# PEER decoding with the sixteen choices innermost, index rows spread by ScalarE, in the slot of spent scores

## The chip, the cores and the metric

The kernel runs on one core of one Trainium2 chip. The metric is the device time of one execution in microseconds (us); the kernel before takes 2549.07 us, the median of 3 runs (2547.81 to 2551.14). Engines: PE is TensorE (matmuls; PEld its weight loads), DVE is VectorE, ACT is ScalarE, POOL is GpSimd, SP is SyncE, which here only issues DMAs.

## The reference

One layer of a hybrid block for 1024 tokens of width 1024. First two mixers (an RG-LRU and an S5 scan) and an output product are added to the residual. Then comes PEER, a product-key lookup of experts, 128 per token (8 heads by 16) out of 16384:

```python
q = (xb @ wq).reshape(TOK_BLOCK, PEER_HEADS, PEER_QDIM)
s1 = einsum('thd,kd->thk', q[..., :PEER_HALF], k1)
s2 = einsum('thd,kd->thk', q[..., PEER_HALF:], k2)
v1, i1 = lax.top_k(s1, 16)
v2, i2 = lax.top_k(s2, 16)
cand = v1[..., :, None] + v2[..., None, :]          # 16 x 16 per head
sc, cidx = lax.top_k(cand.reshape(..., 256), 16)
e = take_along_axis(i1, cidx // 16) * 128 + take_along_axis(i2, cidx % 16)
g = softmax(sc)
act = gelu(einsum('thkd,td->thk', u_tab[e], xb))
out = einsum('thk,thkd->td', g * act, v_tab[e])
```

The change is in the line `e = ...`: of each head, sixteen chosen positions cidx are turned into indices by looking each one up in a list of sixteen (i1 and i2). This is called the decode below.

## The kernel before, in words

The mixers take the first 440 us of the profiled execution. The rest is `peer`. The 1024 tokens are 8 blocks of 128 (a token to a partition), worked in two ways:

- Blocks 5 to 7 are *gathered*. For each of a token's 128 experts POOL's indirect DMA (`ask`, L1380) fetches a row of u, and later of v, for all 128 tokens of the block at once; DVE multiplies and adds (tiles `row`, `act`, `hb`). These are 768 units of one DVE product each, and eight row buffers.
- Blocks 0 to 4 (640 tokens) are *dense*: PE computes all experts. The first product `ap` needs the split weights `uh` (ACT) and `ul` (DVE) of the loaded `ur` (L1461); its gelu goes to the tile `aa` (ACT) and, for 97 of 128 expert tiles, is stored ahead to DRAM (`A_d`, L1559). A half of such a tile is a *step* of 24 matmuls. The weights of the chosen experts are made for every four tokens (a *group*, in `build`) from one-hots `ohA` (DVE) and `ohB` (DVE and ACT) by matmuls `gp`; eight groups fill a tile `gs`, which four DMAs store to `G_d` (L1325). The one-hots of a block need the tile `kt`, the block's transposed indices and weights. After all groups the dense loop runs, which reads `A_d` and `G_d` back.

Which experts a token gets is found as follows. `query` multiplies the tokens by the query weights (loaded as `wqr`, split into `wqh` by ACT and `wql` by DVE; the matmuls `qp`), part 0 for the gathered blocks, part 1 for the dense ones, and makes scores `sp`, 256 per head. Block 0's scores are copied by ACT into the tile `s` (tag "s" of pool `pk`, one buffer, 8 KB a partition), a head at a time; those of blocks 1 to 4 go to DRAM (`S_d`) and are loaded back into the same tile `s` later, 1 MB each (L1205). The largest sixteen of each half are searched by DVE (`top16`: MAX8, FIND_INDEX8 and MATCH_REPLACE8, five operations for one row of 128): `found_g` for the gathered blocks, `search0` for block 0, and the loop in `topk` for blocks 1 to 4. `topk(b)` goes on with 80 candidate sums (`cd`), their top sixteen, a softmax (`ex`), and the chosen positions in the two lists (`pa_`, `pb_`). Then for each of the two halves comes the decode: an `is_equal` of each position with 0 to 15 (`i16`), a multiplication by the sixteen indices `ib`, and four adds that sum over the sixteen (8, 4, 2 and 1 wide), the last into the f32 tile `if`. The tile `oh` of 128 choices by 16 has a slot of its own (4 KB).

The order of the instructions is set by `Merge`, which interleaves generators by modelled costs while the kernel is built: a generator yields, with a condition where it must wait (`search0` waits for a head's scores), and the one whose modelled time is lowest goes on. The framework's scheduler then orders each engine by priority and readiness, also ahead of the chip. On the chip each engine runs its fixed row of instructions in order. `choose` runs `topk` for the dense blocks: block 0's by count of steps, block n's so that its k-th part comes at group 32(n-1)+k. `topks` runs it for the gathered blocks. `build` lets group g go once 23+g steps are done. All engine operations are recorded under L146, a helper's line, so tiles are the names to go by.

Of the kernel before, what the change touches and what calls it, by code (L numbers as in the profile page):

```python
# [9 lines left out]
BF = mybir.dt.bfloat16  # L10
I32 = mybir.dt.int32
U32 = mybir.dt.uint32
AF = mybir.ActivationFunctionType
ALU = mybir.AluOpType
# [4 lines left out]
P = 128  # L19
# [9 lines left out]
def bc(ap, pos, n):  # L29
    shape = list(ap.shape)  # L30
    v = ap.unsqueeze(pos)
    shape.insert(pos, n)
    return v.to_broadcast(shape)
# [1008 lines left out]
def peer(tc, a, cst, pools, h, nx, mg):  # L1042
# [3 lines left out]
    V, S, G, PE = mg.V, mg.S, mg.G, mg.PE  # L1046
    ident, iota = cst["ident"], cst["iota"]
# [103 lines left out]
    def top16(x, vals, at, pin=False):  # L1151
        for r in range(2):
            vs = vals[:, 8 * r:8 * r + 8]
            ins = V.max(vs, x)
            if pin and r == 0:
                tc.keep_in_program_order(ins)
            V.max_index(at[:, 8 * r:8 * r + 8], vs, x)
            if r == 0:
                V.match_replace(x, vs, x, -3.0e38)
# [18 lines left out]
    gp = pools.open("gp", "right", bufs=2)  # L1178
    pu = pools.open("pu", "right", bufs=2)
    pk = pools.open("pk", "right", bufs=1)  # L1180
    i16 = pk.tile([P, 16], BF, name="i16")
    V.tensor_copy(i16, iota[:, 0:16])


    def search0():
# [11 lines left out]
    def topk(b):  # L1197
        if b >= ND:
            yield "found"
            v, ix = found[b - ND]  # L1200
        elif b == dblocks[0]:
            v, ix = s0.pop()
        else:
            s = pk.tile([P, 8, 2, P], F32, name="s", tag="s", bufs=1)
            nc.sync.dma_start(s, S_d[b].rearrange("p h (f k) -> p h f k", f=2))  # L1205
            mg.at(mg.dma(1024))
            yield
            v = pk.tile([P, 2, 8, 16], F32, name="v", tag="v")
            ix = pk.tile([P, 2, 8, 16], U32, name="ix", tag="ix")
            for h in range(8):  # L1210
                for f in range(2):
                    top16(s[:, h, f], v[:, f, h], ix[:, f, h])
                yield

        cd = pk.tile([P, 8, 80], F32, name="cd", tag="cd")
        v1, v2 = v[:, 0], v[:, 1]
        V.tensor_tensor(cd[:, :, 0:16], v2, v1[:, :, 0:1].to_broadcast([P, 8, 16]), ALU.add)
        V.tensor_tensor(cd[:, :, 16:72].rearrange("p h (a b) -> p h a b", b=8), bc(v1[:, :, 1:8], 3, 8),
                        bc(v2[:, :, 0:8], 2, 7), ALU.add)
        V.tensor_tensor(cd[:, :, 72:80], v1[:, :, 8:16], v2[:, :, 0:1].to_broadcast([P, 8, 8]), ALU.add)  # L1220
        sc = pk.tile([P, 8, 16], F32, name="scv", tag="scv")
        ci = pk.tile([P, 8, 16], U32, name="ci", tag="ci")
        for h in range(8):
            top16(cd[:, h], sc[:, h], ci[:, h])
            yield

        ex = pk.tile([P, 8, 16], F32, name="ex", tag="ex")
        V.tensor_tensor(ex, sc, sc[:, :, 0:1].to_broadcast([P, 8, 16]), ALU.subtract)
        yield
        S.activation(ex, ex, AF.Exp)  # L1230
        yield
        sm = pk.tile([P, 8], F32, name="sm", tag="sm")
        V.tensor_reduce(sm, ex, AX.X, ALU.add)
        V.reciprocal(sm, sm)
        g = gw[b - ND].rearrange("p (h k) -> p h k", k=16) if b >= ND else \
            pk.tile([P, 8, 16], F32, name="gd", tag="gd")
        V.tensor_tensor(g, ex, bc(sm, 2, 16), ALU.mult)

        ri = pk.tile([P, P], I32, name="ri", tag="ri")
        cif = ci.rearrange("p h k -> p (h k)").bitcast(I32)  # L1240
        V.tensor_scalar(ri, cif, 3, None, ALU.arith_shift_right)
        V.tensor_scalar(cif, cif, 7, None, ALU.bitwise_and)
        rf = pk.tile([P, P], F32, name="rf", tag="rf")
        cf = pk.tile([P, P], F32, name="cf", tag="cf")
        t9 = pk.tile([P, P], F32, name="t9", tag="t9")
        V.tensor_copy(rf, ri)
        V.tensor_copy(cf, cif)
        V.scalar_tensor_tensor(t9, rf, 9.0, cf, ALU.is_equal, ALU.mult)
        V.tensor_tensor(cf, cf, t9, ALU.subtract)
        pa_ = pk.tile([P, P], BF, name="pa_", tag="pa")  # L1250
        pb_ = pk.tile([P, P], BF, name="pb_", tag="pb")
        t1 = ri.bitcast(F32)
        V.tensor_scalar(t1, rf, 1.0, 8.0, ALU.is_equal, ALU.mult)
        V.tensor_tensor(pb_, cf, t1, ALU.add)
        V.tensor_scalar(rf, rf, -1.0, 0.0, ALU.add, ALU.max)
        V.tensor_tensor(pa_, rf, t9, ALU.add)
        yield
        ib = pk.tile([P, 2, 8, 16], BF, name="ib", tag="ib")
        V.tensor_copy(ib, ix)
        res = []  # L1260
        for f, pos in ((0, pa_), (1, pb_)):
            oh = pk.tile([P, P, 16], BF, name="oh", tag="oh")
            V.tensor_tensor(oh, bc(pos, 2, 16), bc(i16, 1, P), ALU.is_equal)
            oh4 = oh.rearrange("p (h k) a -> p h k a", k=16)
            yield
            V.tensor_tensor(oh4, oh4, bc(ib[:, f], 2, 16), ALU.mult)
            yield
            for m in (8, 4, 2):
                V.tensor_tensor(oh[:, :, 0:m], oh[:, :, 0:m], oh[:, :, m:2 * m], ALU.add)
            o = pk.tile([P, P], F32, name=f"if{f}", tag=f"if{f}")  # L1270
            V.tensor_tensor(o, oh[:, :, 0], oh[:, :, 1], ALU.add)
            res.append(o)
            yield
        return res[0], res[1], g

    def topk_gather(b):
        i1, i2, g = yield from topk(b)
        n = b - ND
        V.scalar_tensor_tensor(i1, i1, 128.0, i2, ALU.mult, ALU.add)
        V.tensor_copy(idx[n], i1)  # L1280
        mg.flag(f"g{n}")
        yield
# [4 lines left out]
    kts, groups, steps = {}, [0], [0]  # L1287

    def choose():
        for n, b in enumerate(dblocks):  # L1290
            found_ = topk(b)
            k = 0
            while True:
                try:
                    next(found_)
                except StopIteration as e:
                    i1, i2, g = e.value
                    break
                k += 1
                at = P // 4 * (n - 1) + k if n else BEGIN + RATE * k  # L1300
                yield lambda: (groups if n else steps)[0] >= at
            p_ = pt("gt")
            for m, x in enumerate((i1, i2, g.rearrange("p h k -> p (h k)"))):
                PE.transpose(p_[:, m * P:(m + 1) * P], x, ident)
            yield
            kt = pk2.tile([P, 5, P], F32, name="kt", tag="kt", bufs=KT)
            V.tensor_copy(kt[:, 0:3], p_[:, :3 * P].rearrange("p (a b) -> p a b", b=P))
            V.tensor_scalar(kt[:, 3:5], kt[:, 1:3], -1.0, None, ALU.mult)
            kts[b] = kt
            mg.flag(f"k{b}")  # L1310
            yield
        mg.flag("k")
# [273 lines left out]

    pace[0] = PACE
    mg.add([(0.0, build()), (0.0, choose()), (1.0, ahead())])
    mg.run([], until="k")
    pools.close("pk")  # L1590
# [283 lines left out]
def body(tc, a):  # L1874
    nc = tc.nc
    pools = Pools(tc)
    pcst = pools.open("cst")
    ident = pcst.tile([P, P], F32, name="ident")
    make_identity(nc, ident)
    iota = pcst.tile([P, P], F32, name="iota")  # L1880
    nc.gpsimd.iota(iota, pattern=[[1, P]], base=0, channel_multiplier=0, allow_small_or_imprecise_dtypes=True)
    mg = Merge(nc)
    cst = dict(ident=ident, iota=iota)
    fpools, h, nx = front(tc, a, cst, ND, mg)
    peer(tc, a, cst, fpools, h, nx, mg)
    pools.close("cst")
# [65 lines left out]
```

## Time and profile before

| | us |
|---|---|
| median of 3 runs | 2549.07 |
| the profiled execution | 2566.11 |
| its span | 2564.3 |
| PE busy | 2490.0 |
| DVE busy | 2361.0 |
| ACT busy | 1336.8 |
| POOL busy | 1193.1 |

The profiled execution is 0.7% longer than the median of the timed ones. In the profile each instruction is named by its engine, its operation and the tiles it writes and reads (`oh<-oh,ib`), with partitions by elements and the element type; a group of equal ones by count, busy us and mean ns of one. A wait `A <- B` is idle time of an engine ahead of instructions that write A, ended by B.

### The profile page before, as it was taken

The page shows a single profiled execution, that of the slowest core. Times are in us where ns is not written, and L with a number is a line of the kernel's source. Part 1 is how long each engine was busy: PE and PEld are TensorE (multiplying, and loading weights), DVE is VectorE, ACT ScalarE, POOL GpSimd, SP SyncE. Part 2 cuts the span into 40 slices and gives each one's busy share as a digit, 9 for nine tenths or more (in the row PEclk, how much of TensorE's full clock was granted, in tenths as well). Part 3 has the DMA queues.
Part 4 walks back from the last instruction along what each step waited for, and adds up shares of the span by engine and source line. Part 5 has one row for each costly group of instructions (what it writes and reads, how often), then busy time and mean ns, then how long its engine had stood idle before and what let it go on. Part 6 is the DMA issues. An engine that isn't in the chain of part 4 may idle for free.

```text
span 2564.3 us, 40749 instructions
## 1 busy us (share of the span) xinstructions
PE 2490.0 (97%) x14639; PEld 2258.2 (88%) x14639; DVE 2361.0 (92%) x4496; ACT 1336.8 (52%) x2388; POOL 1193.1 (47%) x853
## 2 busy tenths in 40 slices
PE   9999999999999999999999999999999999999997
PEld 8777889999989989999999888888888888888886
DVE  8899569999999999999977699999999999999998
ACT  6667334333577777777877344343344344333442
POOL 4000000364467575566555465555556556555551
PEclk9899999999999999999999999999999999999999
DMA  5113124677899989999999999999999999999994
GB/s 191 30 41 130 58 93 157 205 261 271 285 384 328 361 301 324 349 349 310 386 350 351 355 375 356 348 353 356 357 351 367 357 356 351 349 360 355 348 354 150
DMA packets 300906, 750.68 MB, mean 293 GB/s; under 512 B 29600, under 2 KB 127072, under 8 KB 296096
## 3 DMA queue, kind: packets, MB, share of 16 engines
q0 software_dynamic: 112896, 411.09, 43.8%
q1 hardware_dynamic: 185280, 334.19, 36.9%
q10 hardware_dynamic: 2528, 2.80, 0.3%
q8 instruction: 115, 1.88, 0.3%
q14 instruction: 87, 0.71, 0.1%
HBM read 661.87 MB, written 84.93 MB: 291 GB/s over the span
## 4 chain that ended last, share of the span: by engine, by line
PE 61%; DVE 28%; DMA 5%; issue 4%; ACT 2%; POOL 0%; SPq 0%; DVEq 0%; ACTq 0%; POOLq 0%
PE vp L146 26%; PE ap L146 18%; PE total L146 7%; DVE hb L146 5%; PE wop L146 3%; DVE row L146 3%; DVE ul L146 2%; PE gp L146 2%; PE qp L146 2%; DVE ohA L146 2%; DVE oh L146 1%; DMA ur<-in_uT_dram 1%; DVE ix L146 1%; DVE v L146 1%; DVE ci L146 1%
## 5 line engine op out<-in xcount | busy, mean ns | idle before, releaser
L1380 POOL DMA_INDIRECT row<-in_peer_u_dram,idx x384 | 589.1, 1534 | 665.1 <-DVE scv L146 243.8
L1380 POOL DMA_INDIRECT row<-in_peer_v_dram,idx x384 | 567.6, 1478 | 450.7 <-DVE hb L146 264.6
L146 PE MATMUL ap<-xDl,uh 128*128 128x320 f32 x2048 | 649.4, 317 | 7.4 <-ACT aa L146 7.3
L146 PE MATMUL ap<-xDh,ul 128*128 128x320 f32 x2048 | 635.7, 310 | 4.4 <-DVE ul L146 4.4
L146 PE MATMUL ap<-xDh,uh 128*128 128x320 f32 x2048 | 635.1, 310 | 0.0
L146 DVE SCALAR_TENSOR_TENSOR hb<-row,act,hb 128x1024 f32<-128x1024 f32 x384 | 492.5, 1283 | 10.7 <-DMA row<-in_peer_v_dram,idx 5.8
L146 DVE CUSTOM_DVE_ANT_0 row<-row,xg 128x1024 f32<-128x1024 f32 x384 | 458.5, 1217 | 5.1 <-DMA row<-in_peer_u_dram,idx 4.8
L146 PE MATMUL vp<-vl,hh 128*128 128x512 f32 x1024 | 398.8, 389 | 0.0
L146 PE MATMUL vp<-vh,hl 128*128 128x512 f32 x1024 | 398.7, 389 | 0.0
L146 PE MATMUL vp<-vh,hh 128*128 128x512 f32 x1024 | 398.6, 389 | 0.0
L146 PEld LDWEIGHTS ap<-xDl,uh 128*128 128x128 f32 x2048 | 387.9, 189 | 10.2 <-ACT aa L146 9.1
L146 PEld LDWEIGHTS ap<-xDh,ul 128*128 128x128 f32 x2048 | 387.5, 189 | 6.7 <-DVE ul L146 5.4
L146 PEld LDWEIGHTS ap<-xDh,uh 128*128 128x128 f32 x2048 | 386.9, 189 | 0.0
L146 ACT ACTIVATE gq<-gt 128x640 f32<-128x640 f32 x128 | 174.7, 1365 | 318.3 <-DVE hr L146 302.5
L146 PEld LDWEIGHTS vp<-vh,hh 128*128 128x128 f32 x1024 | 192.2, 188 | 40.2
L146 PEld LDWEIGHTS vp<-vl,hh 128*128 128x128 f32 x1024 | 192.2, 188 | 39.3 <-issue 0.4
L146 PEld LDWEIGHTS vp<-vh,hl 128*128 128x128 f32 x1024 | 192.2, 188 | 38.8
L146 ACT ACTIVATE ohB<-ohB,kt 128x128 f32<-128x128 f32 x480 | 201.6, 486 | 0.0
L146 PE MATMUL gp<-ohB,ohA 128*128 128x128 f32 x1280 | 172.7, 278 | 20.6 <-DVE ohB L146 14.0
L146 PEld LDWEIGHTS gp<-ohB,ohA 128*128 128x128 f32 x1280 | 160.8, 192 | 28.4 <-issue 10.4
L146 DVE TENSOR_TENSOR ul<-ur,uh 128x1024 fp32r<-128x1024 f32 x128 | 155.8, 1218 | 22.7 <-ACT uh L146 22.7
L146 ACT ACTIVATE aa<-ap 128x320 f32<-128x320 f32 x194 | 84.4, 436 | 175.3 <-PE ap L146 170.0
(451 smaller groups left out, 4466.5 us busy)
## 6 DMA issues: line engine op xcount, KB each, us to landing
ur<-in_uT_dram SPq DMA_DIRECT2D x128, 512.0 KB, 6.5
vr<-in_peer_v_dram SPq DMA_DIRECT2D x128, 512.0 KB, 7.0
gt<-G_d SPq DMA_DIRECT2D x32, 1280.0 KB, 10.1
G_d<-gs SPq DMA_DIRECT2D x79, 512.0 KB, 10.6
A_d<-aa SPq DMA_DIRECT2D x96, 320.0 KB, 7.4
hr<-A_d SPq DMA_DIRECT2D x96, 320.0 KB, 6.0
wqr<-in_wq_dram SPq DMA_DIRECT2D x31, 512.0 KB, 3.7
row<-in_peer_u_dram,idx POOLq DMA_INDIRECT x384, 7.6
```

What stands on the lines that cost most here:

```text
L146: return fn(*args, **kw)
L1380: G.indirect_dma_start(out=r, out_offset=None, in_=a["peer_v" if at >= P else "peer_u"], in_offset=bass.IndirectOffsetOnAxis(ap=idx[n][:, ...
```

## The change

The decode's tile is turned round, and moved:

- The tile of a half is now [8 heads, 16 slots, 16 choices]: the sixteen choices of a head lie innermost, and the sixteen list positions (slots) outside them. `ia` holds each number 0 to 15 sixteen times over; the compare takes the positions `pos` as they lie, repeated over the slots.
- ACT spreads the sixteen indices of each head over the choices (`ibx`, 128x2048, bf16), once for each half: the first time ahead of `cd`, the second between the first half's multiplication and its adds. The cast to `ib` comes earlier. The multiplication is of two whole tiles.
- The four adds sum over the slots, in runs of sixteen choices.
- `oh` and `ibx` together take 8 KB under the tag "s": the one buffer that holds the scores of block 0 and then those of blocks 1 to 4. The 4 KB of the old tile `oh` are gone.
- In `choose`, block n from 1 on begins its `topk`, whose first instruction is the load of its scores, only at group 32(n-1)-2.

```diff
-    i16 = pk.tile([P, 16], BF, name="i16")
-    V.tensor_copy(i16, iota[:, 0:16])
+    ia = pk.tile([P, 16, 16], BF, name="ia")
+    V.tensor_copy(ia, bc(iota[:, 0:16], 2, 16))
...
+        ib = pk.tile([P, 2, 8, 16], BF, name="ib", tag="ib")
+        V.tensor_copy(ib, ix)
+        both = pk.tile([P, 2, 8, 16, 16], BF, name="oh", tag="s", bufs=1)
+        oh, ibx = both[:, 0], both[:, 1]
+        S.activation(ibx, bc(ib[:, 0], 3, 16), AF.Copy)
         cd = pk.tile([P, 8, 80], F32, name="cd", tag="cd")
...
-        ib = pk.tile([P, 2, 8, 16], BF, name="ib", tag="ib")
-        V.tensor_copy(ib, ix)
         res = []
         for f, pos in ((0, pa_), (1, pb_)):
-            oh = pk.tile([P, P, 16], BF, name="oh", tag="oh")
-            V.tensor_tensor(oh, bc(pos, 2, 16), bc(i16, 1, P), ALU.is_equal)
-            oh4 = oh.rearrange("p (h k) a -> p h k a", k=16)
-            yield
-            V.tensor_tensor(oh4, oh4, bc(ib[:, f], 2, 16), ALU.mult)
-            yield
+            V.tensor_tensor(oh, bc(pos.rearrange("p (h k) -> p h k", k=16), 2, 16), bc(ia, 1, 8), ALU.is_equal)
+            yield
+            V.tensor_tensor(oh, oh, ibx, ALU.mult)
+            yield
+            if f == 0:
+                S.activation(ibx, bc(ib[:, 1], 3, 16), AF.Copy)
             for m in (8, 4, 2):
                 V.tensor_tensor(oh[:, :, 0:m], oh[:, :, 0:m], oh[:, :, m:2 * m], ALU.add)
             o = pk.tile([P, P], F32, name=f"if{f}", tag=f"if{f}")
-            V.tensor_tensor(o, oh[:, :, 0], oh[:, :, 1], ALU.add)
+            V.tensor_tensor(o.rearrange("p (h k) -> p h k", k=16), oh[:, :, 0], oh[:, :, 1], ALU.add)
...
         for n, b in enumerate(dblocks):
             found_ = topk(b)
             k = 0
+            if n:
+                yield lambda: groups[0] >= P // 4 * (n - 1) - 2
             while True:
```

(`bc(x, pos, n)` repeats x over a new axis of length n at place pos.) The whole order of the instructions shifts with this: since `oh` is now a tile of the tag "s", the copy of block 0's first scores stands behind the last add of block 5's decode; the decode of blocks 6 and 7, which lay among the queries' products, stands behind the last search of block 0's scores; block 1's load of scores stands behind the last add of block 0's decode; and the loads of blocks 2 to 4 stand behind a set of four stores to `G_d` rather than ahead of it. Blocks 5 and 0 keep their places to within a few instructions, and the dense loop's order is the same.

## Prediction

> **What bounds the kernel now.** First the page's head and its busy times, then the engines' busy times by stage, because this kernel has stages with different limits.
>
> ```profile
> span 2564.3 us, 40749 instructions
> PE 2490.0 (97%) x14639; PEld 2258.2 (88%) x14639; DVE 2361.0 (92%) x4496; ACT 1336.8 (52%) x2388; POOL 1193.1 (47%) x853
> core 0: us, PE busy (x) PEld busy (x) DVE busy (x) ACT busy (x) POOL busy (x), PEclk, DMA share, GB/s
> 440.00:592.00 152.00, 146.48 (x1006) 143.27 (x1006) 148.01 (x558) 47.79 (x99) 66.40 (x41) 0.99 0.64 217
> 592.00:659.00 67.00, 62.64 (x422) 61.57 (x422) 67.00 (x237) 17.97 (x28) 27.61 (x21) 1.00 0.84 291
> 659.00:760.00 101.00, 94.07 (x642) 91.84 (x641) 95.58 (x254) 66.83 (x160) 67.06 (x45) 0.97 0.96 350
> 760.00:1245.00 485.00, 469.01 (x3344) 462.81 (x3343) 478.93 (x1159) 377.37 (x908) 297.93 (x166) 1.00 0.96 335
> 1245.00:1450.00 205.00, 201.94 (x1448) 201.10 (x1447) 149.96 (x252) 143.75 (x337) 102.73 (x71) 1.00 1.00 355
> 1450.00:2564.00 1114.00, 1098.88 (x5378) 947.65 (x5377) 1058.45 (x1206) 447.23 (x500) 594.97 (x426) 0.99 0.93 345
> ```
>
> The stages are the rest of the queries (440 to 592 us), block 0's choice (to 659), block 0's routing groups (to 760), the choices of blocks 1 to 4 (to 1245), groups alone (to 1450), and the dense loop. From 1245 on PE is busy for 201.94 of 205 us and 1098.88 of 1114, so nothing that VectorE saves there can shorten the run. In the four stages ahead, where all the decoding lies, both engines are nearly full: VectorE is idle for 152 + 67 + 101 + 485 less 148.01, 67.00, 95.58 and 478.93, which is 15.5 us, and PE for 5.5 + 4.4 + 6.9 + 16.0 = 32.8 us. PE's 32.8 us are the most that a lighter VectorE can give back. Whether it does depends on the waits, of which PE's largest in the groups' stages (690 to 1260 us) are these, with total, count and mean or longest in us:
>
> ```profile
> PE gp L146 <- DVE ohB L146: 14.0, 20, 2.5
> PE gp L146 <- ACT ohB L146: 5.2, 3, 3.3
> ```
>
> PE does wait for VectorE, by 14 us at the one-hots ohB, and ACT's own ohB holds it up for 5.2 us more.
>
> **The change part by part.** *1, the decode on VectorE.* A half decode is a compare, a multiplication and four adds. The groups by shape (busy us, mean ns), and the first and last of the sixteen compares (minimum, median and maximum ns):
>
> ```profile
> L146 DVE TENSOR_TENSOR oh<-oh,ib 128x2048 bf16<-128x2048 bf16 x16 | 19.7, 1233 | 0.0
> L146 DVE TENSOR_TENSOR oh<-oh 128x1024 bf16<-128x1024 bf16 x16 | 11.1, 694 | 0.0
> L146 DVE TENSOR_TENSOR oh<-oh 128x256 bf16<-128x256 bf16 x16 | 7.7, 480 | 0.0
> L146 DVE TENSOR_TENSOR oh<-oh 128x512 bf16<-128x512 bf16 x16 | 7.6, 472 | 0.0
> L146 DVE TENSOR_TENSOR if<-oh 128x128 f32<-128x128 bf16 x16 | 7.0, 435 | 0.0
> L146 DVE TENSOR_TENSOR oh<-pa__4501,i x1: 2282/2282/2282, 465.3 to 465.3; 128x2048 bf16<-128x2048 bf16 x1
> L146 DVE TENSOR_TENSOR oh<-pb__13460,i x1: 2290/2290/2290, 1229.7 to 1229.7; 128x2048 bf16<-128x2048 bf16 x1
> ```
>
> The compare takes 2.28 us and the multiplication of the same 2048 bf16 elements 1.23. The compare's first operand repeats one position over its innermost run; after the change every operand of both steps over neighbouring bf16 elements, so I give the compare the multiplication's row: 1.05 us less. The adds of 1024 and 512 differ by 222 ns for 512 elements, 0.43 ns each; carried on from 472 ns this gives 0.36 us for 256, where the row shows 0.48 (runs of two): 0.12 less. The last add reads single elements two apart and takes 0.435; by the same step neighbours would take some 0.31: 0.13 less. The add of 512 I leave, but for 0.02. So 1.05 + 0.02 + 0.12 + 0.13 = 1.32 us a half, and for 8 blocks by 2 halves 21 us. Bounds: nothing at all if the comparison doesn't speed up and short runs don't matter, and 24 us if all adds gain. I take 21, since the multiplication's row is the same size and type.
>
> The Trainium skill, "VectorE: DVE Perf Modes", What auto-detection actually checks, says that two elements a cycle need every tensor to be 16-bit with step one, and names no length of the run. By it the 256 add was fast already and the last add, which writes f32, never is, so 16 times 1.05 = 16.8 us would go and the sum below be 4 us higher. The 480 ns beside 472 for twice the elements speaks against it for short runs.
>
> *2, ACT's sixteen spreads of 128x2048.* No row shows one. The nearest on both sides:
>
> ```profile
> L146 ACT ACTIVATE wqh<-wqr 128x1024 fp32r<-128x1024 f32 x31 | 32.6, 1052 | 1.5 <-DMA wqr<-in_wq_dram 1.5
> L146 ACT ACTIVATE gq<-gt 128x640 f32<-128x640 f32 x128 | 174.7, 1365 | 318.3 <-DVE hr L146 302.5
> ```
>
> Doubling the first less one fixed part gives 1.9 to 2.1 us; at the second's 2.13 ns an element it would be 4.4 us. I take 2, for the elements read lie side by side in bf16: 32 us in all, half of them (four blocks) between 760 and 1245 where ACT is busy for 377 of 485 us. VectorE needs the first spread only after cd, eight top-16 searches and the softmax, and the second after the adds and the next compare, so it is not waited for. If that cover is gone, each spread holds up an aa or an ohB behind it by 2 us (4.4 at the bound): up to 16 us for the eight in this stage.
>
> *3, the queries' stage.* The decode now lives in the slot of the scores s. Of blocks 6 and 7 it can therefore not begin before block 0's scores are searched. VectorE's row around block 6's decode, before the change (pa is the position, row the gathered rows, wql the low part of query weights):
>
> ```order
> L146 CAST ib<-ixg_3348 128x256
> L146 TENSOR_TENSOR oh<-pa__4786,i_4319 128x2048
> L146 ISA row,act<-row,xg 128x1024
> L146 ISA act 128x1
> L146 TENSOR_TENSOR oh<-oh,ib 128x2048
> L146 TENSOR_TENSOR wql<-wqr,wqh 128x1024
> ```
>
> And after it, where the last operations on s are still block 0's searches:
>
> ```order
> L146 MATCH_REPLACE s<-v,s 128x128 x2
> L146 MAX v<-s 128x8 x2
> L146 MAX_INDEX ix<-v,s 128x8 x2
> L146 TENSOR_TENSOR cd<-v 128x8x16
> L146 TENSOR_TENSOR oh<-pa__4855,ia 128x2048
> L146 TENSOR_TENSOR cd<-v 128x8x56
> L146 TENSOR_TENSOR pa__5270<-rf,t_5265 128x128
> L146 TENSOR_TENSOR oh<-oh 128x2048
> ```
>
> So two decodes, 2 x 2 x (2.28 + 1.23 + 0.69 + 0.47 + 0.48 + 0.44) = 22 us by before's rows, leave the stretch ahead of the last head's search. The timeline there (start, us):
>
> ```profile
> 570.66 1.21 DVE L146 TENSOR_TENSOR wql<-wqr,wqh 128x1024 fp32r<-128x1024 f32 x1
> 582.01 0.38 ACT L146 ACTIVATE s<-sp 128x256 f32<-128x256 f32 x1
> 590.92 0.28 DVE L146 FIND_INDEX8 ix<-v,s 128x8 uint32<-128x128 f32 x1
> 640.37 0.40 DVE L146 TENSOR_TENSOR if<-oh 128x128 f32<-128x128 bf16 x1
> 658.55 0.54 DVE L146 COPY kt<-gt 128x384 f32<-128x384 f32 x1
> ```
>
> PE, which makes these scores with 5.5 us idle in 152, can't follow by 22 us: the scores come at 582.0, or at best some 5 us sooner. VectorE takes up four more gather products (39 instead of 35, 5 us) in the freed time and stands at this head's search at about 572 to 574: it then waits 8 to 12 us. I take 10, bounds 3 (the scores come 5.5 sooner) and 12. Its search then ends at about 585 instead of 591.
>
> The slot also ties block 0's first scores to block 5's decode, whose last add stands here:
>
> ```profile
> L146 DVE MAX8 v<-s x160: 261/276/305, 566.7 to 1164.9; 128x8 f32<-128x128 f32 x160
> 458.71 0.38 ACT L146 ACTIVATE s<-sp 128x256 f32<-128x256 f32 x1
> 474.97 0.44 ACT L146 ACTIVATE qt<-qp 128x320 f32<-128x320 f32 x1 [3.08 <-PE qp L146]
> 477.79 0.39 DVE L146 TENSOR_TENSOR if<-oh 128x128 f32<-128x128 bf16 x1
> ```
>
> With 2.6 us saved this add ends at 475.6, so the copy slips by 17 us, in ACT's row to just ahead of the qt of 474.97, which it can hold up by a microsecond. VectorE's first search of s comes at 566.7 only, so I cost this at nothing; without that cover PE's next query product waits 1 us.
>
> *4, block 1's scores.* Their load waited for nothing but block 0's search; now it waits for the last add of block 0's decode. The loads of the four blocks' scores (first and last issue; us to landing):
>
> ```profile
> L1205 SPq DMA_DIRECT2D s<-S_d x4: 319/319/319, 591.2 to 1018.8; - x4
> DMA to landing us min/median/max: 6.4/7.3/8.0
> ```
>
> That add stood at 640.4; with search done 6 us sooner, the two decodes of part 3 put in (17 us as they now cost) and 2.6 us saved it comes at about 648. VectorE's row behind it, after the change (if is the decoded index, ul a split of dense weights):
>
> ```order
> L146 TENSOR_TENSOR oh<-oh 128x8x32
> L146 TENSOR_TENSOR if_6625<-oh 128x128
> L146 ISA row,act<-row,xg 128x1024
> L146 ISA act 128x1
> L146 TENSOR_TENSOR ul<-ur,uh 128x1024
> L146 MAX v<-s 128x8 x2
> L146 MAX_INDEX ix<-v,s 128x8 x2
> L146 MATCH_REPLACE s<-v,s 128x128 x2
> ```
>
> Only a gather product and a ul split, some 2.4 us, cover the 7.3 us to landing: VectorE waits about 5 us there (bounds 0, if the load is hoisted by a gather that is late, and 8). Before, the search of block 1 was mixed with this decode. Of the 80 search operations 20 instead of 53 now stand ahead of kt, on which the groups rest, so kt keeps its place to within 3 us of 658.55.
>
> *5, the scores of blocks 2 to 4.* SP's row at block 4, before (ur is dense weights, G_d and A_d the stores of groups and of the first product):
>
> ```order
> L1461 DMA ur<-in_uT_dram 128x1024
> L1205 DMA s<-S_d 128x2048
> L1325 DMA G_d<-gs 128x8x128
> L1559 DMA A_d<-aa 128x640
> L1325 DMA G_d<-gs 128x8x128 x3
> ```
>
> And after:
>
> ```order
> L1466 DMA ur<-in_uT_dram 128x1024
> L1330 DMA G_d<-gs 128x8x128 x3
> L1564 DMA A_d<-aa 128x640
> L1330 DMA G_d<-gs 128x8x128
> L1205 DMA s<-S_d 128x2048
> L1466 DMA ur<-in_uT_dram 128x1024
> ```
>
> The new wait for a count of groups moves the load behind a whole set of four stores, and so it is with blocks 2 and 3. Block 4's set on SP in before, what a load right behind it needed, where the search stands; the same for block 3; a store's size and usual landing, and the landings of the slowest set:
>
> ```profile
> 1091.63 4.04 SPq L1325 DMA_DIRECT2D G_d<-gs  x3
> 1097.19 1.36 SPq L1325 DMA_DIRECT2D G_d<-gs  x1
> 1099.93 0.34 SPq L1461 DMA_DIRECT2D ur<-in_uT_dram  x1
> DMA to landing us min/median/max: 11.3/11.3/11.3
> 1105.45 0.48 DVE L146 MAX8 v<-s 128x8 f32<-128x128 f32 x2
> 943.92 0.45 SPq L1325 DMA_DIRECT2D G_d<-gs  x1
> 958.55 0.48 DVE L146 MAX8 v<-s 128x8 f32<-128x128 f32 x2
> G_d<-gs SPq DMA_DIRECT2D x79, 512.0 KB, 10.6
> DMA to landing us min/median/max: 11.3/17.8/18.1
> ```
>
> Issued at 1098.6 and landing 11.3 us later the scores are there at 1110, and the search is due at 1105.5: 4.5 us (3 to 6). The search of block 3 stands 14 us behind its set (944.4 to 958.55): 0 to 3; block 2's I take as 0 as well. All together 4.5 us, and 15 if the three land like the slowest stores at 18 us.
>
> *The sum:* -21 + 10 + 5 + 4.5 = -1.5 us on VectorE, which sets the pace there. The profiled execution took 2566.11 us (span 2564.3), 0.67% above the median of 2549.07; the difference is carried to the median without scaling: 2547.5 us.
>
> **The rivals.** About 0.2%, 5 us, is what a measurement of this kernel can tell from no change.
> - *Forecast, no change* (2544 to 2554): the savings are eaten by waits for scores. Chance 0.37.
> - *The saving reaches the end.* Where parts 3 and 5 cost little, because the earlier query weights bring PE's last scores forward by its 5.5 us and the loads land before they are due, -21 + 5 = -16 us remain, 2533. For it: PE waits 14 us for VectorE's ohB and 32.8 us are there to be had. Against: an order fixed ahead gives VectorE little to do in its new waits. Chance 0.36. The Trainium skill, "Perfetto Trace Analysis", Optimizing Scalar/DVE Operations, says that handing work to the scalar engine may make sense where VectorE is saturated; by that this case would be the one.
> - *Slower: scores late behind stores.* Each load of scores now queues behind 2 MB of stores. At 18 us to landing blocks 2 to 4 cost 15 us instead of 4.5: -21 + 10 + 5 + 15 = +9, 2558; with two spreads of ACT in the way of ohB a block, +13, 2562. It decides once block 4's scores need over 14 us from issue (block 3's over 17). For it: the DMA share of 0.96 there and the 18.1 us. Against: the 11.3. Chance 0.22.
> - *It doesn't do what it says:* the compare stays at 2.28 us. Then only 16 x 0.27 = 4 us go and the sum is +15, 2564. Against it stands the multiplication's row. Chance 0.05.
>
> **How the numbers follow.** Faster by over 0.2% 0.36, the same 0.37, slower 0.22 + 0.05 = 0.27. The likeliest case gives 2547.5. The range runs from 2533 (the gain in full) to 2561 (late scores, with some of ACT's cost); the full +15 and a gain over 16 us are left out.
>
> **What would show it.** In the profile after: compares near 1.23 us, last adds near 0.31; spreads near 2 us on ACT; an idle stretch of VectorE at about 572 to 582 that ends with s<-sp; one of about 5 us that ends with a load of s near 650; landings of the s loads of over 7.3 us at blocks 2 to 4; VectorE's last decode near 1245. I am wrong if these waits are missing and the last decode ends 10 us sooner, or if PE's idle time from 440 to 1245 doesn't follow VectorE's.

## The result: slower by 0.9%

The changed kernel takes 2576.2 us, the median of 6 runs (2573.2 to 2578.7), beside 2551.8 for the kernel before (6 runs, 2547.8 to 2558.8): a ratio of 1.0093, 95% interval 1.0080 to 1.0105. The prediction was 2547.5 us with a range of 2533 to 2561, so it was wrong.

The profiled execution of before that the prediction quotes was a long one (2566.1 us). Below, the changed kernel is held against a second profile of before, from the control run (span 2553.7 us); the control's own timed rounds were disturbed and gave no ratio. The stages of the changed kernel (PE, PEld, DVE, ACT and POOL busy us, clock, DMA share, GB/s):

```profile
440.00:592.00 152.00, 148.13 (x1026) 144.82 (x1026) 140.26 (x568) 55.90 (x104) 61.89 (x47) 1.00 0.68 241
592.00:659.00 67.00, 62.43 (x406) 61.57 (x404) 58.78 (x171) 25.93 (x36) 21.29 (x16) 0.95 0.73 244
659.00:760.00 101.00, 94.31 (x659) 91.73 (x660) 101.00 (x299) 69.29 (x163) 69.05 (x44) 1.00 0.96 336
760.00:1245.00 485.00, 457.66 (x3238) 452.55 (x3237) 458.11 (x1151) 372.48 (x879) 254.88 (x163) 0.98 0.95 330
```

The same of the control, that is of the kernel before:

```profile
440.00:592.00 152.00, 145.47 (x1008) 142.32 (x1007) 151.44 (x569) 47.72 (x99) 64.34 (x43) 1.00 0.66 222
592.00:659.00 67.00, 63.99 (x430) 62.70 (x428) 67.00 (x237) 20.56 (x36) 27.76 (x20) 1.00 0.82 280
659.00:760.00 101.00, 96.56 (x674) 95.44 (x675) 96.39 (x257) 68.50 (x163) 68.98 (x46) 0.98 0.98 361
760.00:1245.00 485.00, 472.68 (x3379) 467.58 (x3379) 484.76 (x1169) 379.80 (x916) 292.83 (x169) 1.00 0.96 340
```

From 760 to 1245 us PE is idle for 27.3 us instead of 12.3, and VectorE, which was full, for 26.9. The loss is made between the first and the last of the tiles kt, before (control) and after:

```profile
L146 DVE COPY kt<-gt x5: 540/559/573, 655.5 to 1240.5; 128x384 f32<-128x384 f32 x5
```

```profile
L146 DVE COPY kt<-gt x5: 547/555/573, 656.7 to 1260.1; 128x384 f32<-128x384 f32 x5
```

The first comes 1.2 us later, the last 19.6, of the 20.4 us by which the spans differ (2553.7 and 2574.1). So nearly the whole loss lies between the two tiles. What VectorE waited for in the changed kernel, in the queries' stage and block 0's choice (440 to 659), and then from 760 on, with PE's wait that grew:

```profile
DVE v L146 <- ACT s L146: 8.6, 1, 8.6
DVE v L146 <- DMA s<-S_d: 5.0, 1, 5.0
...
DVE v L146 <- DMA s<-S_d: 26.6, 3, 10.7
PE gp L146 <- DVE ohB L146: 25.6, 13, 8.2
```

PE's wait for ohB in the same stretch of the control:

```profile
PE gp L146 <- DVE ohB L146: 8.2, 13, 2.0
```

The 8.6 and the 5.0 us are those of parts 3 and 4 of the prediction; they lie ahead of the first kt, which is only 1.2 us late, so that what VectorE saved there paid for them. The 26.6 us at the searches of blocks 2 to 4 are far above the 4.5 of part 5, in three waits of up to 10.7 us; behind each of them stand one-hots, and PE's longest wait for ohB went from 2.0 to 8.2 us. The decode itself became as cheap as forecast, and more (one compare, the groups by shape, and ACT's spreads):

```profile
L146 DVE TENSOR_TENSOR oh<-pa__7988,ia x1: 1217/1217/1217, 768.0 to 768.0; 128x2048 bf16<-128x2048 bf16 x1
L146 DVE TENSOR_TENSOR oh<-oh 128x2048 bf16<-128x2048 bf16 x16 | 19.5, 1220 | 0.0
L146 DVE TENSOR_TENSOR oh<-oh 128x1024 bf16<-128x1024 bf16 x16 | 11.0, 685 | 0.0
L146 DVE TENSOR_TENSOR oh<-oh 128x512 bf16<-128x512 bf16 x16 | 6.7, 418 | 0.1
L146 DVE TENSOR_TENSOR oh<-oh 128x256 bf16<-128x256 bf16 x16 | 4.6, 287 | 0.1
L146 DVE TENSOR_TENSOR if<-oh 128x128 f32<-128x128 bf16 x16 | 4.6, 285 | 0.1
L146 ACT ACTIVATE oh<-ib x16: 1894/1910/1911, 451.2 to 1239.8; 128x2048 bf16<-128x2048 bf16 x16
```

A half went from 2.28 + 1.23 + 0.69 + 0.47 + 0.48 + 0.44 = 5.59 us to 1.22 + 1.22 + 0.69 + 0.42 + 0.29 + 0.29 = 4.13: 1.46 less, 23 us in all (21 were forecast; VectorE's whole busy time fell by 21.5, from 2361.0 to 2339.5). Against the control VectorE's whole busy time fell by 20.1 us (from 2359.6), so its ledger is -20.1 + 8.6 + 5.0 + 26.6 = +20.1 us, beside 20.4 us in the traces and 24 in the timed runs. On PE's side 16.3 of the 20.4 us are idle time; the other 4.1 are longer matmuls (2490.8 us busy instead of 2486.7 for the same 14639), at a mean granted clock of 0.988 instead of 0.992. The lower clock is seen in the stages 592 to 659 and 760 to 1245 us (0.95 and 0.98, in the control 1.00).

Why the scores came late is to be seen on SP at block 4 (start, us that the issue took; the last line is of all four loads of scores):

```profile
1093.58 5.25 SPq L1330 DMA_DIRECT2D G_d<-gs  x3
1098.92 2.81 SPq L1564 DMA_DIRECT2D A_d<-aa  x1
1101.78 1.21 SPq L1330 DMA_DIRECT2D G_d<-gs  x1
1103.09 2.03 SPq L1205 DMA_DIRECT2D s<-S_d  x1
DMA to landing us min/median/max: 8.7/13.5/15.0
```

And the searches that waited for the three loads, on VectorE:

```profile
812.95 0.49 DVE L146 MAX8 v<-s 128x8 f32<-128x128 f32 x2 [5.55 <-DMA s<-S_d]
961.12 0.49 DVE L146 MAX8 v<-s 128x8 f32<-128x128 f32 x2 [10.71 <-DMA s<-S_d]
1116.12 0.49 DVE L146 MAX8 v<-s 128x8 f32<-128x128 f32 x2 [10.37 <-DMA s<-S_d]
```

The load of block 4 was issued at 1103.1, not 1098.6: the set of stores began 2.0 us later than in the first profile of before, and SP took 9.4 us to issue it (with the A_d store in it) instead of 6.9. It landed 13.0 us later; the search stood ready at 1105.7, as forecast. For block 3 the search stood ready at 950.4, 8 us sooner than in the first profile of before but 2 us later than in the control's (948.1), and the load (issued at 946.1) took 15.0 us; for block 2 the same three numbers are 807.4, 798.9 and 14.0.

### The profile page after: what moved, and what is told of

Same layout as the page of the kernel before. It is cut to its first block, busy times and chain, and to the rows that moved or that the text cites. A ratio compares the mean times of both kernels' runs of the same rounds, so it can differ in the third digit from the quotient of the medians.

```text
span 2574.1 us, 40763 instructions
## 1 busy us (share of the span) xinstructions
PE 2490.8 (97%) x14639; PEld 2260.2 (88%) x14639; DVE 2339.5 (91%) x4496; ACT 1362.4 (53%) x2404; POOL 1147.6 (45%) x853
## 4 chain that ended last, share of the span: by engine, by line
PE 63%; DVE 26%; DMA 6%; issue 3%; ACT 2%; SPq 0%; DVEq 0%; ACTq 0%
PE vp L146 26%; PE ap L146 17%; PE total L146 6%; DVE hb L146 5%; PE qp L146 5%; PE wop L146 3%; DVE ul L146 2%; PE gp L146 2%; DVE row L146 2%; DMA s<-S_d 2%; DVE ohA L146 2%; DVE oh L146 1%; DVE ix L146 1%; DVE v L146 1%; DVE ohB L146 1%
## 5 line engine op out<-in xcount | busy, mean ns | idle before, releaser
L1385 POOL DMA_INDIRECT row<-in_peer_u_dram,idx x384 | 564.2, 1469 | 687.8 <-DVE act L146 265.5
L1385 POOL DMA_INDIRECT row<-in_peer_v_dram,idx x384 | 547.2, 1425 | 482.1 <-DVE hb L146 264.5
L146 DVE TENSOR_TENSOR h<-h,vp 128x1024 f32<-128x1024 f32 x128 | 155.7, 1216 | 19.2 <-PE vp L146 17.8
```

What stands on the lines that cost most here:

```text
L146: return fn(*args, **kw)
L1385: G.indirect_dma_start(out=r, out_offset=None, in_=a["peer_v" if at >= P else "peer_u"], in_offset=bass.IndirectOffsetOnAxis(ap=idx[n][:, ...
```

## The experiments

Theory W: the shared slot makes the loads of scores late, and VectorE's waits for them cost the time. Rivals: ACT's sixteen spreads hold up aa and ohB (A); the moved decodes and searches ahead of 760 us (O). All ratios are to the kernel before, run on the same chip.

**Control.** The kernel before, unchanged.

> The kernel before, once more, against itself. The one profiled execution of before took 2566.1 us where its runs lie about 2551.8; the changed kernel's profile fits its runs (2575.9 beside 2576.2). Both theories expect a ratio of 1.000 within 0.002, and a profiled span near 2550 us, with the 14 us less spread thinly or in one stage: that stage then has to be read from this profile and not from the first.

The profiled span is 2553.7 us, near the 2550 expected, and the difference to the first profile lies thinly in several stages (PE is idle for 26.3 us from 440 to 1245 instead of 32.8).

**The slot alone.** Against the kernel before.

```diff
+        both = pk.tile([P, 2, P, 16], BF, name="oh", tag="s", bufs=1)
...
-            oh = pk.tile([P, P, 16], BF, name="oh", tag="oh")
+            oh = both[:, f]
...
+            if n:
+                yield lambda: groups[0] >= P // 4 * (n - 1) - 2
```

> The slot alone: before's decode (choices outermost, one tile of 128x16 after another, no spreads on ACT) in the slot of the scores, with the new wait for a count of groups. Theory W (the slot makes the loads of scores late, and VectorE waits for them: 8.6 + 5.0 + 26.6 = 40 us in the changed kernel's profile, against 21.5 us that the decode saves): these waits stay at 30 to 45 us and nothing is saved, 2576 + 21 = 2597 us, at least 2585. Rival A (ACT's sixteen spreads hold up aa and ohB and so PE): no spreads, so 2552 to 2560.

Measured: 2573.0 us, 1.0068 (1.0045 to 1.0092). The sharing costs without any spread, against rival A, but not as theory W had it, which asked for at least 2585: in its profile VectorE waits 7.4 us for block 0's last scores and only 2.3 for loads, since the searches of blocks 2 to 4 come only after their scores have landed (block 4's land at 1117.7 us, its search begins at 1119.8). Instead PE lost time behind the two decodes that the slot pushed past the searches:

```profile
607.32 0.64 PE L146 MATMUL ap<-xDh,ul 128*128 128x320 f32 x1 [10.97 <-DVE ul L146]
```

The first kt comes at 662.8 us here, 7.3 later than in the control. From 760 on another 6.2 us of PE's time are lost (18.5 us idle instead of 12.3), while VectorE waits 7.5 us for gathered rows; why is not shown. So the slot has a second price, order: the decodes of blocks 6 and 7 stand in one piece, from 582.3 to 603.3 us, ahead of a split that PE needs (in the changed kernel, with cheaper decodes, that wait is 3.8 us).

**The layout alone.** Against the changed kernel: a slot of its own for oh; the spread in halves of four heads in the slot of `cd`.

```diff
-        both = pk.tile([P, 2, 8, 16, 16], BF, name="oh", tag="s", bufs=1)
...
+            oh = pk.tile([P, 8, 16, 16], BF, name="oh", tag="oh")
...
-            V.tensor_tensor(oh, oh, ibx, ALU.mult)
+            for q in (0, 4):
+                ibx = pk.tile([P, 4, 16, 16], BF, name="ibx", tag="cd")
+                S.activation(ibx, bc(ib[:, f, q:q + 4], 3, 16), AF.Copy)
+                V.tensor_tensor(oh[:, q:q + 4], oh[:, q:q + 4], ibx, ALU.mult)
...
-            if n:
-                yield lambda: groups[0] >= P // 4 * (n - 1) - 2
```

> The layout alone: the new decode with its tile oh in a slot of its own (4 KB as before), the spread indices in halves of four heads in the slot of the spent candidate sums, the decoded indices in two other spent tiles, and no wait for a count of groups. Theory W: no wait of VectorE for a load of scores over 1 us; the decode saves 21.5 us less 16 x (2 x 0.69 - 1.22) = 2.6 for the halved multiplication, so 19 us of VectorE; PE gets most of it: 2533 us (2528 to 2542). Rival A: the spreads are still there (32 of half the size), so 2565 or more.

Measured: 2553.3 us, 0.9993 (0.9981 to 1.0004). No wait for a load is left, and it is some 23 us faster than the changed kernel; but the 19 us that the decode saves bring nothing: neither theory W's 2533 nor rival A's 2565. In its stretch from 760 on VectorE now stands idle for 14.7 us, which it wasn't before, 7.5 of them behind PE's gp and 6.6 behind gathered rows, and PE is idle for 15.0 us, not less than the control's 12.3:

```profile
760.00:1245.00 485.00, 470.02 (x3360) 465.52 (x3360) 470.33 (x1161) 386.27 (x922) 263.88 (x168) 1.00 0.97 340
DVE ohA L146 <- PE gp L146: 7.5, 6, 2.3
```

**The changed kernel without the wait for a count of groups** (the two lines in `choose` taken out).

> The changed kernel without the new wait for a count of groups: the loads of blocks 2 to 4 are issued as soon as the slot is free, one or two of the four stores later than which they were issued behind. Theory W: the wait of 26.6 us at blocks 2 to 4 shrinks to 8 to 16 us, the ones of 8.6 and 5 us stay, 2560 us (2553 to 2567). Rival A: no change, 2576.

Measured: 2562.2 us, 1.0034 (1.0020 to 1.0049). The issues go from 798.9, 946.1 and 1103.1 to 792.5, 939.3 and 1088.7, and the waits for all four loads from 31.6 to 17.5 us:

```profile
DVE v L146 <- DMA s<-S_d: 17.5, 4, 6.6
```

14 us less waiting and 14 us less time, against rival A.

**The late loads alone.** Before, with its own slots; the loads of blocks 2 to 4 held where the changed kernel has them.

```diff
-            nc.sync.dma_start(s, S_d[b].rearrange("p h (f k) -> p h f k", f=2))
+            ins = nc.sync.dma_start(s, S_d[b].rearrange("p h (f k) -> p h f k", f=2))
+            if b > dblocks[1]:
+                tc.keep_in_program_order(ins)
...
+            if n:
+                yield lambda: groups[0] >= P // 4 * (n - 1)
```

> The late loads alone: the kernel before with its own decode and slots, in which the loads of the scores of blocks 2 to 4 stand where the changed kernel has them, behind a whole set of four stores (one load of ur later than there); block 1's load stands as before. Theory W (late scores are the cost): VectorE waits 20 to 30 us for them, PE's idle time from 760 to 1245 us goes from 12 to about 25, and the time to 2562 to 2570 us. Rival O (the loss comes from the moved decodes and searches ahead of 760 us): no more than 2556.

Measured: 2571.2 us, 1.0080 (1.0063 to 1.0096). PE's idle time in the stretch is 26.8 us, as expected:

```profile
760.00:1245.00 485.00, 458.24 (x3263) 451.50 (x3262) 469.88 (x1141) 367.35 (x883) 273.16 (x163) 1.00 0.96 333
DVE v L146 <- DMA s<-S_d: 11.0, 2, 5.7
```

Late loads alone make nearly the whole loss, without spreads or moved decodes: against A and O. The time is a little above the expected range, and the wait shown is smaller than expected: 11 us, 15.1 of idle time with that for gathered rows, beside 14.8 us by which the profiled span (2568.5 us) is longer than the control's.

**More of VectorE's work.** The compare of each block's first half done twice.

```diff
             V.tensor_tensor(oh, bc(pos, 2, 16), bc(i16, 1, P), ALU.is_equal)
+            if f == 0:
+                V.tensor_tensor(oh, bc(pos, 2, 16), bc(i16, 1, P), ALU.is_equal)
```

> More of VectorE's decode: the kernel before with the compare of each block's first half done twice, 8 x 2.28 = 18.2 us more on VectorE, the same result. Theory P (PE sets the pace in these stages and VectorE's work is worth nearly nothing while it comes in small pieces; so the 19 us that the layout alone saved brought nothing): at most 2557 us. Rival V (VectorE sets the pace, and the layout's gain was eaten by ACT's spreads): 2566 to 2572.

Measured: 2569.4 us, 1.0061 (1.0038 to 1.0084), some 16 us for 18.2 of work: theory P falls. VectorE is full there, and more costs its time:

```profile
760.00:1245.00 485.00, 469.27 (x3332) 459.58 (x3331) 485.00 (x1165) 374.07 (x903) 301.63 (x166) 1.00 0.95 335
```

**ACT's work alone.** Before, with the 32 half spreads, read by nobody.

```diff
+            for q in (0, 4):
+                ibx = pk.tile([P, 4, 16, 16], BF, name="ibx", tag="cd")
+                S.activation(ibx, bc(ib[:, f, q:q + 4], 3, 16), AF.Copy)
             V.tensor_tensor(oh4, oh4, bc(ib[:, f], 2, 16), ALU.mult)
```

> ACT's work alone: the kernel before with the 32 half spreads of the layout-alone run added (128x1024, 1.05 us each, 34 us of ACT), written and read by nobody. Rival V (these spreads stand in the way of aa and ohB and eat 19 us): 2562 to 2571. Theory P: at most 2555.

Measured: 2551.0 us, 1.0004 (0.9994 to 1.0014). The spreads are there, but hidden: rival A falls, and with it half of rival V.

```profile
L146 ACT ACTIVATE ibx<-ib x32: 1038/1056/1081, 461.3 to 1203.7; 128x1024 bf16<-128x1024 bf16 x32
```

This run has halves; of the changed kernel's whole spreads its own profile says the same: from 760 to 1245 us PE waits 1.8 us for ACT's ohB and aa there, in the control 3.7.

**The loads on another queue.** The changed kernel, with `S.dma_start(s, ...)` for `nc.sync.dma_start(s, ...)`.

> The changed kernel with the loads of scores issued by ACT's queue instead of SP's, at the same places of the program. If the ring order behind the stores makes the scores late, they land within 9 us again instead of 13.0 to 15.0, VectorE's wait at blocks 2 to 4 falls from 26.6 to 10 us or less, and the time to about 2562. If the DMA engines are simply full (share 0.95), landing stays at 12 us or more and the time at 2572 to 2578.

Measured: 2556.1 us, 1.0016 (1.0006 to 1.0026), 20 us faster than the changed kernel with one word changed. The loads (issue, landing) and what is left of the wait from 760 on:

```profile
L1205 ACTq DMA_DIRECT2D s<-S_d x4: 326/330/340, 644.7 to 1093.8; - x4
DMA to landing us min/median/max: 9.3/9.5/9.6
DVE v L146 <- DMA s<-S_d: 2.6, 1, 2.6
```

They are issued in 0.33 us instead of 2 to 3, block 4's 9 us sooner, and land in about 9.5 (block 2's landing is not in the trace) instead of 13.0 to 15.0, with the DMA engines as full as before (share 0.97). A wait of 8.5 us of VectorE for ACT's uh from 760 on is new here. The queue behind the stores was the delay, not the engines' load alone. The Trainium skill, "DMA: Bandwidth & Descriptors", Queues, rings and completion order, says that SP and ACT each have rings of their own on the same DMA engines and that on each engine descriptors are consumed in ring order; this pair of runs agrees.

**Less of VectorE's work, and nothing else.** Why the layout alone gained nothing was open; this takes 18.2 us off VectorE in almost before's own order. The kernel leaves out the lookup of half of each index, so the rows that it gathers are other ones.

```diff
-            V.tensor_tensor(oh, bc(pos, 2, 16), bc(i16, 1, P), ALU.is_equal)
+            if f == 0:
+                V.tensor_tensor(oh, bc(pos, 2, 16), bc(i16, 1, P), ALU.is_equal)
...
-            V.tensor_tensor(oh4, oh4, bc(ib[:, f], 2, 16), ALU.mult)
+            V.tensor_tensor(oh4, bc(bc(i16, 1, 16), 1, 8) if f else oh4, bc(ib[:, f], 2, 16),
+                            ALU.is_equal if f else ALU.mult)
```

> Less of VectorE's decode and nothing else: the kernel before without the compare of each block's second half (left out, so that half of the index is not looked up: an equality of the sixteen indices with 0 to 15 stands in the multiplication's place, of the same size and speed). 8 x 2.28 = 18.2 us less on VectorE, in almost the same order. Theory T1 (both engines are full there, so more work on VectorE costs its time, as the doubled compare did, but less soon meets PE's own limit): 2546 to 2551 us, at most 5 us gained. Theory T2 (VectorE sets the pace both ways, and the layout-alone run lost its 19 us to its own order or to the split spreads): 2532 to 2541.

Measured: 2553.7 us, 0.9992 (0.9980 to 1.0004). T1: the work is gone and the time isn't. What VectorE does with it:

```profile
760.00:1245.00 485.00, 473.60 (x3397) 470.00 (x3397) 471.55 (x1149) 379.15 (x916) 274.48 (x172) 1.00 0.97 343
DVE ohA L146 <- PE gp L146: 9.9, 7, 2.3
PE ap L146 <- ACT aa L146: 5.5, 3, 2.4
PE gp L146 <- DVE ohB L146: 4.8, 9, 1.8
```

It is idle for 13.5 us and mostly waits for PE; PE's idle time, 11.4 us beside 12.3, hardly moves. But what PE waits for has changed: 4.8 us for VectorE's ohB instead of 8.2, and 5.5 for ACT's aa instead of 0.4. By the profiles PE got some of VectorE's time and lost it to another wait; no run takes work off ACT, and what holds PE's idle time at 11 to 15 us stays open.

**Fewer, and more, gather products beside the groups, with the layout alone.**

```diff
-FIRST, STEP, KT, LEAD = 72, (1.6, 1.6), 2, 23
+FIRST, STEP, KT, LEAD = 72, (1.5, 1.5), 2, 23
```

> The layout alone with fewer gather products beside the groups: 1.5 for each step instead of 1.6, some 16 units or 20 us of VectorE moved into the dense loop, where VectorE is idle for about 48 of 1090 us. T1: PE's waits are single ones behind one-hots, not VectorE's load: 2548 to 2554. T2: VectorE's load still sets PE's waits of 10 us for ohB: 2540 to 2545.

Measured: 2551.9 us, 0.9989 (0.9975 to 1.0003), T1. With (1.7, 1.7):

> The same with more: 1.7 for each step, some 16 units or 20 us more on VectorE beside the groups. If the layout freed time that VectorE now spends waiting (14.7 us idle from 760 to 1245, behind gp and gathered rows), they cost little: 2553 to 2558 (T1). T2: 2565 or more.

Measured: 2547.4 us, 0.9976 (0.9967 to 0.9986): faster than both kernels, by 0.24% than before, where both theories expected a loss. The 0.24% are hardly more than the 0.2% that a measurement of this kernel can tell. VectorE is nearly full again, and PE idle for 12.6 us, in the control 12.3:

```profile
760.00:1245.00 485.00, 472.40 (x3388) 467.01 (x3387) 482.98 (x1189) 389.11 (x925) 277.17 (x181) 1.00 1.00 358
```

**The kernel before with 1.7**, to see whether that gain is the layout's.

> The kernel before with 1.7 gather products for each step, its own decode: is the gain of 0.24% in the run of the layout with 1.7 that of the layout, or of the 1.7? T1 (the layout frees VectorE time that only counts once other work is put in it): VectorE is full here, 20 us more cost 10 to 18 us, 2562 to 2570, as the doubled compare did. Rival: the 1.7 alone brings it (fewer products in the dense loop): 2545 to 2550.

Measured: 2564.4 us, 1.0052 (1.0034 to 1.0071): T1. The 1.7 costs 13 us with the old decode and nothing with the new one. With 1.7 the two decodes are 17 us apart (2564.4 and 2547.4), near the 19 us of VectorE that the layout saves: there the saving is paid out.

## Why the prediction was wrong

- **Part 1, the decode:** right. The compare took 1.22 us (1.23 forecast), the 256 add 0.29 (0.36), the last add 0.29 (0.31), the saving was 23 us by these rows and 20.1 in VectorE's whole busy time (21). The last add of the kernel before reads single elements sixteen apart, not two as the prediction has it. The rule of the Trainium skill weighed there ("VectorE: DVE Perf Modes", What auto-detection actually checks) would have left the 256 and the last add as they were; they fell from 480 to 287 ns with runs of 32 (two slots by sixteen choices) in place of two, and from 435 to 285 with runs of sixteen in place of one, and the measurement decides.
- **Part 2, the spreads:** right. 1.91 us each (2 forecast), hidden; shown by ACT's work alone (in halves) and by PE's waits in the changed kernel.
- **Part 3:** right in its wait (8.6 us, 10 forecast) and in the slip of the first copy of s (475.2 us).
- **Part 4:** right (5.0 us, 5 forecast; the first kt within 2 us of where it stood).
- **Part 5 failed:** "All together 4.5 us, and 15 if the three land like the slowest stores" measured 26.6. The mechanism was named, and it was the rival *scores late behind stores* that came true, with 26.6 in the place of its 15. Four things were mis-sized. Block 2's wait was taken as 0 with no row for it and was 5.6: in the first profile of before its set of stores ends at 797.7 us and the row of its searches begins at 805.3, so block 4's 11.3 us would already have given 4. The landing was taken as 11.3 us and was 13.0 to 15.0. The issue was read off the end of the stores in before's profile, but the queue that makes a landing late also makes SP late: at block 4 the load went out 4.5 us later, 2.5 of them longer issues of the stores and 2.0 a later start of the set. And block 3's 14 us between its set and its search were those of one long execution: in the control they are 6.6 (941.5 to 948.1), in the changed kernel 4.4 (946.0 to 950.4), and its wait, taken as 0, was 10.7.
- **The sum's frame failed too:** "-1.5 us on VectorE, which sets the pace there". More work or waits on VectorE do cost their time (doubled compare, late loads), but less work gives nothing (compare left out, layout alone): PE's idle time stayed at 11 to 15 us of 485, the control's being 12.3, while VectorE began to wait for it. That PE is as good as full there is inferred from this; which of its waits would have to go is not shown. So the rival *the saving reaches the end*, with 0.36, would not have come true even with every load on time: the layout alone has them on time and gains nothing, so its "32.8 us are there to be had" were not. In this order a saving was only set off against waits or other work.

What stays open: why 1.7 with the new layout is faster than before by 6 us and not only equal (its last kt comes at 1243.0 us, 2.5 later than the control's, so by these two profiles the gain lies behind it), what holds PE's idle time where it is, and the 4 us between the 20 of the traces and the 24 of the timed runs.

## What to carry to other kernels

A slot that is shared to save space ties a transfer to the end of another tile's life; price the transfer from where it will stand in its queue then, with the landing and the issue time that this queue shows at that place, and against the due time in the new order. Before counting a saving on a full engine, ask what its waits say in the other direction: in this kernel, with a second engine within 3% of full, adding work cost its time and removing it did not pay until other work was moved into the room. Read a slack from more than one execution: the 14 us of one profile were 6.6 in the next. A late load in a crowded queue may be cured by issuing it from another engine's queue.

## What the runs showed of the hardware

- A load of 1 MB behind four stores of 512 KB on SP's queue landed in 13.0 to 15.0 us in the changed kernel and took SP 2.0 to 3.1 us to issue; from ACT's queue at the same places 9.5 to 9.6 us and 0.33. The same loads on SP's queue landed in 8.7 to 14.3 us in the run of the slot alone and in 10.2 to 16.7 in that of the late loads alone, so such a landing scatters widely.
- A bf16 add of 256 elements took 480 ns in runs of two and 287 in runs of 32; one of 128 elements into f32 took 435 ns reading one element in sixteen and 285 reading runs of sixteen neighbours.
- An ACT copy of 128x2048 bf16 that repeats each element sixteen times took 1.91 us, and one of 128x1024 took 1056 ns, beside 1052 for `wqh<-wqr` of the same count, which reads neighbours. Carried on from the rows of 256 (384 ns) and 1024 elements (1052 ns), a plain copy of 2048 would take 1.94 us by estimate, so the repeated reading cost nothing that shows.
